# Reordering VectorE's low parts around the gated tiles of a decoder layer's FFN

## The chip, the cores and the metric

The kernel runs on one core of a Trainium2 chip. The metric is the device time of one execution in microseconds (us), given as the median of several runs. PE is TensorE, DVE is VectorE, ACT is ScalarE, POOL is GpSimd, SP is SyncE, whose queue issues nearly all loads. "L176" is line 176 of the kernel.

## The reference

One decoder layer over 256 tokens of width 1024: a mixer (pooling and attention), a cross-attention into 256 memory tokens, and a gated FFN of inner width 2816, each followed by a layer norm of `alpha * h + branch`. The change touches the FFN:

```python
def swiglu(h, w_gate, w_up, w_down):
    return (jax.nn.silu(h @ w_gate) * (h @ w_up)) @ w_down
...
h = layer_norm(DEEPNORM_ALPHA * h + swiglu(h, w_gate[l], w_up[l], w_down[l]), ln3_g[l], ln3_b[l])
```

All data are float32.

## The kernel before

**High and low parts.** TensorE multiplies in a rounded 32-bit type (fp32r). So every operand is cut in two: ACT casts it to fp32r (the high part, `w101h`), DVE subtracts that from the original (the low part, `w101l`), and a product is the sum of three matmuls (L477 high x high, L478 with the low part, L479). A weight tile is 128 x 1024 elements, 512 KB. It goes through a load into one of 7 raw buffers (`w101r`, issued on SP at L108 or L105), ACT's cast (L160) and DVE's subtraction (L176). The raw buffer of tile i is used again by tile i+7, so the load of w108 waits for the low part of w101.

**The stream of weights.** The class `Stream` numbers the tiles in the order of use. `cast()` emits the load, the cast and, unless `apart` is set or the tile is in `lazy`, one low part; what is cast and not yet subtracted waits in `unsplit`. `prepare(upto)` casts up to a tile and subtracts everything below it. `next()` is called after a step of the products and casts one tile more while fewer than `ahead` tiles are in hand (8, then 10 from chunk 3 on) beyond `used`; it does nothing while `held` is set. `get()` asks for the tile that is needed now and looks one tile further. Instructions stand on each engine in the order in which the program emits them: an engine never takes a later one first.

Some tiles are sums of others. A "fourth" tile (w87, w90, w94, w97, w117, ...) is completed by a DVE addition at L165 before it can be cast; sums that are built in DRAM (`sum_z`, `sum_w`, for the down projection) are begun by SP copies (L428, L433) and completed by accumulating DMAs from POOL (`add_first`, `add_second`, L440), in three thirds.

**The FFN's chunks.** The 2816 inner columns are 11 chunks of 256. Chunk c takes four tiles: chunk 1 w69 to w72, chunk 4 w81 to w84, chunk 7 w99 to w102, chunk 8 w103 to w106, chunk 9 w107 to w110, chunk 10 w111 to w114. `proj_both` runs four row blocks of high parts (L492) and then their low parts (L498), twice; 16 steps. Each chunk fills four PSUM banks (`pg`); chunks alternate between two sets of four. After a chunk, `Gated.add` empties them: ACT copies (L1342), DVE adds (L1343, four sums). In the next chunk `multiply` applies silu on ACT and multiplies on DVE (L1348), and `split` makes the gated tile's sum forms on DVE (`add_forms`, L727 to L729), its cast on ACT (L1361) and its low part on DVE (L1366). For the chunks c from 2 to 4 `split` first asks for one more weight tile, whose low part then stands between that cast and L1366.

**The row chunks.** Chunks 5 and 6 (`ROWS`) are computed together from w85 to w98 in 28 products of three matmuls (`Rows.products`) into seven banks. `leave` empties them: an ACT copy (L1445) and then seven DVE operations (L1447 to L1460), all of which follow, directly or not, from L1445. Chunk 7 takes its four banks over from the first four of these. `multiply` (L1464), eight transposes on TensorE (L1473) and `split` (L1479 to L1485) follow inside chunk 7.

**The down projection.** After chunk 10 TensorE multiplies the gated tiles with w115 to w146 (`summed`, two products a tile), and then with w147 to w150 (`pieces`). Its eight banks are those of chunks 9 and 10; the first four products write to banks of chunk 9, the fifth, with w117, to one of chunk 10. At the end DVE combines the sums and does the layer norm (L1001 to L926).

`make_forms` (L1368) prepares sum forms of h2 for the row chunks in seven steps: four DVE operations of 512 columns, two ACT casts (L1382), two DVE subtractions (L1385).

Of the kernel before, what the change touches and what calls it, by code (L numbers as in the profile page):

```python
# [24 lines left out]
NFC = DFF // CW  # L25
# [18 lines left out]
ROWS = (5, 6)  # L44
# [5 lines left out]
def r32(t):  # L50
    return t.bitcast(F32)


class Stream:
# [137 lines left out]
    def next(self):  # L192

        if not self.held:
            self.prepare(min(self.used + self.ahead, len(self.tiles) + 1))

    def get(self, numbers, k):

# [24 lines left out]
def decoder_layer(  # L223
# [26 lines left out]
    ws = Stream(nc, rp, wp)  # L250
# [110 lines left out]
    def split_xt(k, n=2):  # L361
        split(*xT.parts(k, n), xr[:, k:k + n, :])
# [7 lines left out]
    def split_mem(k):  # L370
        split(*mT.parts(k, 4), mr[0][:, k:k + 4, :])
# [70 lines left out]
    def add_first(i):  # L442
        assert i in sums_begun
        js = slice(i * THIRD, (i + 1) * THIRD)
        add_to(sum_z[:, :, js], w_sum[:, 2:4, js])

    def add_second(i):
        assert ~i in sums_begun
        js = slice(i * THIRD, (i + 1) * THIRD)
        add_to(sum_w[:, js], sum_z[:, 1, js])  # L450
# [33 lines left out]
    def proj_both(pss, numbers, yT, group=KD):  # L484

        for k0 in range(0, KD, group):
            for k in range(k0, k0 + group):
                hi, _ = ws.get(numbers, k)  # L490
                for b, ps in enumerate(pss):
                    nc.tensor.matmul(ps, hi[:, b * P:(b + 1) * P], yT.both(k), start=k == 0, stop=False,  # L492
                                     skip_group_check=True)
                yield
            for k in range(k0, k0 + group):
                _, lo = ws.parts_of(numbers, k)
                for b, ps in enumerate(pss):
                    nc.tensor.matmul(ps[:, S:], lo[:, b * P:(b + 1) * P], yT.pair(k)[0], start=False,  # L498
                                     stop=k == KD - 1, skip_group_check=True)
                ws.done(numbers, k)  # L500
                if ws.pace == 1:
                    ws.next()
                yield
# [31 lines left out]
    def run(gen, n=None):  # L535

        while n is None or n > 0:
            if next(gen, gen) is gen:
                return False
            n = None if n is None else n - 1  # L540
        return True

    def split(h, l, ps):
        nc.scalar.copy(h, ps)
        nc.vector.tensor_sub(l, ps, r32(h))
# [5 lines left out]
    def transpose_tok(dst, tok, t, k0, copy=None):  # L551

        ps = bank("tp")
        for k in range(4):
            nc.tensor.transpose(ps[:, k * P:(k + 1) * P], tok[:, (k0 + k) * P:(k0 + k + 1) * P], ident)
        ts = slice(t * P, (t + 1) * P)
        y = ps.rearrange("p (k t) -> p k t", k=4)
        split(*dst.parts(k0, 4, ts), y)
        if copy is not None:
            nc.scalar.copy(copy[:, k0:k0 + 4, ts], y)  # L560
# [164 lines left out]
    def add_forms(q, eng=nc.vector):  # L725

        eng.tensor_sub(q[..., 4:6, :], q[..., 0:2, :], q[..., 1:4:2, :])  # L727
        eng.tensor_sub(q[..., 6, :], q[..., 5, :], q[..., 0, :])
        eng.tensor_add(q[..., 7, :], q[..., 2, :], q[..., 6, :])  # L729
# [508 lines left out]
    products(1, "w", PLAN["w"][1:])  # L1238
    first = shared.parts(0)
    next(first)  # L1240
    xattend(3, homes[1])
    run(first)
# [14 lines left out]
    ws.used += 2  # L1257
    norm.stats()
    next(second)
    norm.unit()  # L1260

# [33 lines left out]
    def gated_parts(c):  # L1295


        if c in SUMMED:
            t = (late if c == ROWS[-1] + 1 else ap).tile([P, 2, 8, P], F32R, tag="a8", name=f"g{c}")
            gT[c] = t[:, 0], t[:, 1]  # L1300
            return
        if not shared:
            shared.append(ap.tile([P, 2, 8, P], F32R, tag="a8", name="go"))
        j = LAST.index(c)
        gT[c] = tuple(shared[0][:, n, 4 * j:4 * j + 4] for n in range(2))
# [14 lines left out]
    def gated_t():  # L1320
        pt = bank("pgt").rearrange("p (f t) -> p f t", f=2)
        for t in range(T):
            for f in range(2):
                nc.tensor.transpose(pt[:, f, t * P:(t + 1) * P], sg0[:, t, f * P:(f + 1) * P], ident)
        gated_parts(0)
        split(gT[0][0], gT[0][1], pt.rearrange("p f (t s) -> p (f t) s", t=T))

    class Gated:
# [18 lines left out]
            nc.scalar.activation(gate, gate, AF.Silu, bias=0.0, scale=1.0)  # L1347
            nc.vector.tensor_mul(gate, gate, up)  # L1348

        def split(self):  # L1350
            gated_parts(self.c)
            hi, lo = gT[self.c]
            q, n = self.forms, 4
            part = ROWS[0] - 3 <= self.c < ROWS[-1]
            if part:
                ws.apart = True
                ws.more()
            if self.c in SUMMED:
                n = 8
                add_forms(q)  # L1360
            nc.scalar.copy(hi[:, :n], q[:, :n])  # L1361
            if part:
                while ws.unsplit:
                    ws.low()
                ws.apart = False
            nc.vector.tensor_sub(lo[:, :n], q[:, :n], r32(hi[:, :n]))  # L1366

    def make_forms():  # L1368

        q = h2f.rearrange("p (j f) (t s) -> p j f t s", f=2, t=2)  # L1370
        at = {(f, t): q[:, :, f, t] for f in range(2) for t in range(2)}
        nc.vector.tensor_sub(at[1, 1], at[0, 1], at[1, 1])
        yield
        nc.vector.tensor_sub(at[0, 1], at[0, 0], at[0, 1])
        yield
        nc.vector.tensor_sub(at[0, 0], at[1, 1], at[0, 0])
        yield
        nc.vector.tensor_add(at[1, 0], at[1, 0], at[0, 0])
        yield
        halves = [[y[:, j:j + 4] for y in (*extra, h2f)] for j in (0, 4)]  # L1380
        for hi, _, y in halves:
            nc.scalar.copy(hi, y)  # L1382
        yield
        for hi, lo, y in halves:
            nc.vector.tensor_sub(lo, y, r32(hi))  # L1385
            yield
# [114 lines left out]
    left, rows, later = None, None, norms[0].vectors()  # L1501
    extra = [pool.tile([P, KD, S], F32R, tag="a8", name=f"extra{i}") for i, pool in enumerate((late, ap))]
    more_forms = make_forms()
    for c in range(1, NFC):
        if c == ROWS[0]:
            run(more_forms)
            rows = Rows()
            ws.lazy = c_gu[ROWS[-1] + 1]
            gu = rows.products()
            run(gu, 3)  # L1510
            left.multiply()
            run(gu, 3)
            left.split()
            run(gu, 10)
            add_first(1)
            add_second(1)
            ws.held = True
            run(gu)
            left = rows
        if c in ROWS:  # L1520
            continue
        pss = [(accbank if c % 2 else bank)("pg") for _ in range(4)]
        if c == 3:
            ws.ahead += 1
            ws.widen("spare", sp)
            add_second(0)
        if c == 7:
            add_first(2)
            add_second(2)
        ws.held = ws.held or c == ROWS[0] - 1  # L1530
        gu = proj_both(pss, c_gu[c], h2T, KD if c == 1 else 4)
        run(gu, 2)
        if left:
            left.multiply()
        run(gu, 2)
        if left and left is rows:
            run(gu, 3)
            left.transposed()
            left.split()
            ws.held = False  # L1540
        elif left:
            left.split()
            run(more_forms, {2: 4, 3: 1}.get(c, 0))
            if c == ROWS[-1] + 2:
                run(later)
        else:
            run(gu, 4)
            gated_t()
        if c >= 2:
            run(gu, 7 if c < ROWS[0] else 4)  # L1550
            if c == 3:
                run(more_forms, 2)
            ws.held = True
        run(gu)
        left = Gated(c, pss)
        left.add()
        ws.held = False
# [174 lines left out]
```

## Time and profile before

| what | value |
|---|---|
| median of 3 runs | 382.34 us (381.67 to 382.8) |
| profiled execution, its own time | 384.75 us |
| its span, first to last instruction | 382.4 us |
| PE / DVE / ACT busy in the span | 367.8 / 342.0 / 230.9 us |
| mean granted TensorE clock | 0.985 |

The profiled execution takes 2.35 us more than its span, and 2.4 us more than the median of the runs. Busy shares are means over the whole kernel; the FFN runs from about 196 us to the end. A row of a timeline gives start, length, engine, line, operation, output<-input, shape and count, and in brackets how long the engine was idle just before and what ended that.

### The profile page before, as it was taken

The numbers are of one execution on the slowest core, as the hardware profiler recorded it, in microseconds if no ns is written. First come the engines' busy times: TensorE is split into PE (matmuls) and PEld (weight loads), VectorE is DVE, ScalarE is ACT, GpSimd is POOL, SyncE is SP. The second block draws the span as 40 slices with busy tenths as digits, with TensorE's granted clock in tenths as the row PEclk, the third lists the DMA queues.
The fourth block names the chain that finished last, engine by engine and source line by source line (L and its number), as shares of the span: only waits on it lengthen the run. The fifth ranks groups of instructions, "written<-read, shape, count | busy, mean of one in ns | idle before, by whom it ended". The sixth has DMA issues, their size and how long they took to land.

```text
span 382.4 us, 5499 instructions
## 1 busy us (share of the span) xinstructions
PE 367.8 (96%) x1941; PEld 311.4 (81%) x1941; DVE 342.0 (89%) x523; ACT 230.9 (60%) x356; POOL 36.5 (10%) x41
## 2 busy tenths in 40 slices
PE   9999999999999999999999999986999995999994
PEld 8888878888888889988888888863888884888882
DVE  6878899998999999999879897989598989899995
ACT  5767768657262965672487446846395467676602
POOL 0000055500130001001100001000100000000013
PEclk9999999999999999999999999999899997999999
DMA  7999997869769999999989489999999757899502
GB/s 273 411 411 362 221 395 237 342 209 300 285 137 258 393 373 317 282 329 366 284 221 366 159 272 316 279 304 316 401 271 333 237 187 220 275 312 295 191 0 110
DMA packets 33754, 107.58 MB, mean 281 GB/s; under 512 B 3264, under 2 KB 4544, under 8 KB 32320
## 3 DMA queue, kind: packets, MB, share of 16 engines
q1 hardware_dynamic: 31056, 93.41, 67.3%
q0 software_dynamic: 2240, 13.37, 17.8%
q10 hardware_dynamic: 432, 0.46, 0.3%
q8 instruction: 15, 0.25, 0.3%
q14 instruction: 11, 0.09, 0.1%
HBM read 106.18 MB, written 27.79 MB: 350 GB/s over the span
## 4 chain that ended last, share of the span: by engine, by line
PE 65%; DVE 20%; issue 5%; DMA 5%; ACT 4%; DVEq 0%; ACTq 0%
PE pg L492 9%; PE m L477 5%; PE m L478 5%; PE m L479 5%; PE pg L498 4%; PE pxk L492 4%; PE pqk L611 4%; DMA w50r<-in_w_xq 3%; PE x L477 2%; PE pxq L492 2%; PE x L478 2%; PE pqk L614 2%; PE x L479 2%; PE pu L492 2%; PE pxk L498 2%
## 5 line engine op out<-in xcount | busy, mean ns | idle before, releaser
L1361 ACT CAST g<-sq 128x1024 fp32r<-128x1024 f32 x7 | 7.4, 1052 | 21.6 <-DVE sq L729 21.6
L916 POOL TENSOR_TENSOR rs<-mv,mhalf 128x1 f32<-128x1 f32 x6 | 4.4, 726 | 125.5 <-DVE mv L914 125.5
L1366 DVE TENSOR_TENSOR g<-sq,g 128x1024 fp32r<-128x1024 f32 x7 | 8.6, 1226 | 6.7 <-ACT g L1361 6.7
L676 ACT ACTIVATE pr<-pr,mx 128x128 f32<-128x128 f32 (+1 forms) x16 | 7.1, 445 | 7.7 <-DVE mx L707 7.7
L440 POOL DMA_DIRECT2D sum_z<-in_w_sum x3 | 3.2, 1056 | 77.1 <-DMA sum_z<-in_w_sum 77.1
L1347 ACT ACTIVATE sq<-sq 128x512 f32<-128x512 f32 x8 | 5.1, 640 | 7.0 <-DVE sq L1343 7.0
L905 DVE BATCH_NORM_STATS2 st<-r 128x6 f32<-128x512 f32 (+1 forms) x12 | 8.1, 672 | 0.4
L570 ACT ACTIVATE h2f<-tp,turned 128x128 f32<-128x128 f32 x8 | 3.0, 456 | 7.0 <-PE tp L567 7.0
L921 DVE SCALAR_TENSOR_TENSOR r<-r,mv,gb 128x512 f32<-128x512 f32 (+2 forms) x10 | 6.9, 724 | 0.1
L727 DVE TENSOR_TENSOR sq<-sq 128x256 f32<-128x256 f32 x9 | 3.8, 423 | 3.3 <-ACT sq L1479 3.2
L1342 ACT COPY sq<-pg 128x256 f32<-128x256 f32 x16 | 5.1, 368 | 2.2 <-PE pg L498 2.2
L1022 DVE TENSOR_TENSOR r<-r,u 128x512 f32<-128x512 f32 x6 | 6.0, 1016 | 0.1
L819 ACT CAST xkTh<-pxk 128x256 fp32r<-128x256 f32 x8 | 2.6, 377 | 5.7 <-PE pxk L498 5.7
L1343 DVE TENSOR_TENSOR sq<-pg,sq 128x256 f32<-128x256 f32 x16 | 6.0, 418 | 0.0
L1343 DVE TENSOR_TENSOR sg<-pg,sg 128x256 f32<-128x256 f32 x16 | 6.0, 418 | 0.0
L932 ACT ACTIVATE h<-r,rs 128x512 f32<-128x512 f32 x2 | 1.3, 718 | 7.3 <-DVE r L921 7.3
L1348 DVE TENSOR_TENSOR sq<-sq,sg 128x512 f32<-128x512 f32 x8 | 5.5, 691 | 0.2
L1027 DVE TENSOR_TENSOR r<-m,r 128x512 f32<-128x512 f32 (+1 forms) x8 | 5.2, 652 | 0.5 <-PE m L479 0.4
L676 ACT ACTIVATE xpr<-xs,mx 128x256 f32<-128x256 f32 x6 | 2.8, 472 | 4.7 <-DVE mx L687 4.7
L776 POOL TENSOR_TENSOR win<-upad 128x542 f32<-128x542 f32 x2 | 4.0, 1992 | 16.9 <-DVE upad L809 16.9
L440 POOL DMA_DIRECT2D sum_w<-sum_z x3 | 2.6, 851 | 29.2 <-DMA sum_z<-in_w_sum 29.2
L1342 ACT COPY sg<-pg 128x256 f32<-128x256 f32 x16 | 5.3, 389 | 0.0
(1373 smaller groups left out, 1398.7 us busy)
## 6 DMA issues: line engine op xcount, KB each, us to landing
sum_z<-in_w_sum SPq DMA_DIRECT2D x3, 1536.0 KB, 9.5
sum_z<-in_w_sum POOLq DMA_DIRECT2D x3, 1536.0 KB, 14.9
sum_w<-in_w_sum SPq DMA_DIRECT2D x3, 768.0 KB, 11.5
sum_w<-sum_z POOLq DMA_DIRECT2D x3, 768.0 KB, 7.9
gs_z<-in_w_gs SPq DMA_DIRECT2D x1, 2048.0 KB, 9.4
gs_z<-in_w_gs POOLq DMA_DIRECT2D x1, 2048.0 KB, 18.1
wr<-in_w_qkv SPq DMA_DIRECT2D x5, 256.0 KB, 4.8
mr<-in_mem_t SPq DMA_DIRECT2D x1, 1024.0 KB, 11.6
```

The costliest lines, as they stand in the source:

```text
L477: nc.tensor.matmul(ps, wa, ya, start=start, stop=False, skip_group_check=part)
L478: nc.tensor.matmul(ps, wa, yb, start=False, stop=False, skip_group_check=part)
L479: nc.tensor.matmul(ps, wb, ya, start=False, stop=stop, skip_group_check=part)
L492: nc.tensor.matmul(ps, hi[:, b * P:(b + 1) * P], yT.both(k), start=k == 0, stop=False, skip_group_check=True)
L498: nc.tensor.matmul(ps[:, S:], lo[:, b * P:(b + 1) * P], yT.pair(k)[0], start=False, stop=k == KD - 1, skip_group_check=True)
L611: nc.tensor.matmul(qk[i], part(i)[0], xT.both(k), start=first, stop=False, skip_group_check=True)
L614: nc.tensor.matmul(qk[i][:, S:], part(i)[1], x_hi, start=False, stop=last, skip_group_check=True)
L676: nc.scalar.activation(dst[:, j, :], src[:, j, :], AF.Exp, bias=mx[:, j:j + 1], scale=sign, accum_out=sm[:, j:j + 1])
L905: nc.vector.bn_stats(self.st[:, self.n, :], self.r[:, c0:c1] if src is None else src)
L1342: nc.scalar.copy(y[:, f, :], ps[:, S:])
L1343: nc.vector.tensor_add(y[:, f, :], ps[:, :S], y[:, f, :])
L1366: nc.vector.tensor_sub(lo[:, :n], q[:, :n], r32(hi[:, :n]))
```

## The change

It has five parts.

- `next()` calls `more()`, which casts a tile without subtracting everything that is left over. So the lazy tiles (chunk 7's w99 to w102) stay `unsplit` until `get` asks for them, which is after the row chunks' sums.
- `split` may be given work to emit between the cast and L1366 (`fill`): steps of `more_forms` in chunks 2 and 3. The seven steps of `more_forms` are spread anew: two in the gap of chunk 1's gated tile and two behind it, the casts late in chunk 2, one subtraction in the gap of chunk 2's gated tile, one late in chunk 3.
- `split` asks for one more tile for c = 2 to 4 and 7 to 9, instead of 2 to 4 alone. In the row chunks `apart` is set one product ahead of the split of chunk 4's gated tile, so that two tiles (w96, w97) can stand there.
- `held` is set through chunk 10 (`NFC - 1`).
- The DMAs that complete the last third of `sum_z` and `sum_w` are emitted at chunk 9 instead of chunk 7.

```diff
     def next(self):
 
         if not self.held:
-            self.prepare(min(self.used + self.ahead, len(self.tiles) + 1))
+            self.more()
...
-        def split(self):
+        def split(self, fill=None):
             gated_parts(self.c)
             hi, lo = gT[self.c]
             q, n = self.forms, 4
-            part = ROWS[0] - 3 <= self.c < ROWS[-1]
+            part = ROWS[0] - 3 <= self.c < NFC - 1
             if part:
                 ws.apart = True
                 ws.more()
...
             nc.scalar.copy(hi[:, :n], q[:, :n])
+            if fill:
+                run(*fill)
             if part:
                 while ws.unsplit:
                     ws.low()
...
             left.multiply()
-            run(gu, 3)
+            run(gu, 5)
+            ws.apart = True
+            run(gu, 1)
             left.split()
-            run(gu, 10)
+            run(gu, 7)
             add_first(1)
             add_second(1)
             ws.held = True
...
-        if c == 7:
+        if c == 9:
             add_first(2)
             add_second(2)
-        ws.held = ws.held or c == ROWS[0] - 1
+        ws.held = ws.held or c in (ROWS[0] - 1, NFC - 1)
...
         elif left:
-            left.split()
-            run(more_forms, {2: 4, 3: 1}.get(c, 0))
+            left.split((more_forms, 4 - c) if c in (2, 3) else None)
+            if c == 2:
+                run(more_forms, 2)
             if c == ROWS[-1] + 2:
                 run(later)
...
             run(gu, 7 if c < ROWS[0] else 4)
-            if c == 3:
-                run(more_forms, 2)
+            if c < ROWS[0] - 1:
+                run(more_forms, 1)
             ws.held = True
```

## Rows read from the trace of the kernel before

**Rows 1.** The page's chain of work that ended last, by engine.
```profile
PE 65%; DVE 20%; issue 5%; DMA 5%; ACT 4%; DVEq 0%; ACTq 0%
```
**Rows 2.** Busy time by stretch: span, each engine, granted clock, DMA share, GB/s.
```profile
236.00:246.00 10.00, 10.00 (x54) 8.59 (x53) 9.83 (x18) 5.78 (x10) 0.09 (x1) 1.00 1.04 271
...
256.00:266.00 10.00, 6.59 (x24) 4.27 (x24) 9.89 (x10) 6.62 (x8) 0.00 (x0) 1.00 0.95 321
266.00:274.00 8.00, 7.35 (x30) 5.71 (x31) 5.36 (x9) 1.23 (x2) 1.04 (x1) 0.79 1.02 411
...
322.00:324.00 2.00, 2.00 (x6) 1.61 (x5) 2.00 (x3) 1.47 (x2) 0.00 (x0) 0.50 1.05 399
```
**Rows 3.** TensorE's timeline, row chunks to the down projection.
```profile
241.58 0.40 PE L477 MATMUL g<-w86h,h2T 128*128 128x512 f32 x1
...
259.98 0.50 PE L478 MATMUL g<-w97l,extra 128*128 128x512 f32 x1 [0.76 <-DVE w97l L176]
...
266.25 0.50 PE L492 MATMUL pg<-h2T,w99h 128*128 128x512 f32 x1 [1.45 <-DVE row L1447]
...
273.77 1.04 PE L1473 MATMUL pgt<-ident,row 128*128 128x128 f32 x8
...
280.69 2.00 PE L492 MATMUL pg<-h2T,w103h 128*128 128x512 f32 x8
...
314.09 0.40 PE L477 MATMUL m<-w115h,g 128*128 128x512 f32 x1
...
320.95 0.80 PE L477 MATMUL m<-w117h,g 128*128 128x512 f32 x1 [3.96 <-DVE sq L1343]
```
**Rows 4.** VectorE's timeline over the same stretch and the end.
```profile
233.41 1.23 DVE L176 TENSOR_TENSOR w87l<-w87r,w87h 128x1024 fp32r<-128x1024 f32 x1 [1.62 <-ACT w87h L160]
...
244.03 0.75 DVE L1343 TENSOR_TENSOR sq<-pg,sq 128x256 f32<-128x256 f32 x2
...
260.97 1.22 DVE L176 TENSOR_TENSOR w99l<-w99r,w99h 128x1024 fp32r<-128x1024 f32 x1
...
265.51 0.69 DVE L1447 TENSOR_TENSOR row<-g,row 128x512 f32<-128x512 f32 x1
...
275.02 0.42 DVE L727 TENSOR_TENSOR sq<-sq 128x256 f32<-128x256 f32 x1 [3.25 <-ACT sq L1479]
...
317.26 0.69 DVE L1366 TENSOR_TENSOR go<-sq,go 128x512 fp32r<-128x512 f32 x1 [0.69 <-ACT go L1361]
...
357.01 1.23 DVE L176 TENSOR_TENSOR w146l<-w146r,w146h 128x1024 fp32r<-128x1024 f32 x1
...
369.52 0.69 DVE L1027 TENSOR_TENSOR r<-m,r 128x512 f32<-128x512 f32 x1 [0.43 <-PE m L479]
...
375.33 0.43 DVE L905 BATCH_NORM_STATS2 st<-acc 128x6 f32<-128x256 f32 x1 [0.18 <-PE acc L479]
```
**Rows 5.** Groups by line: VectorE's L1366, with the idle time ahead of it.
```profile
L1366 DVE TENSOR_TENSOR g<-sq,g 128x1024 fp32r<-128x1024 f32 x7 | 8.6, 1226 | 6.7 <-ACT g L1361 6.7
```
**Rows 6.** Busy time of all engines between two VectorE instructions of group 4.
```profile
244.03:375.33 131.30, 123.15 (x591) 102.16 (x590) 119.71 (x158) 77.85 (x98) 5.69 (x6) 0.96 0.78 255
```
**Rows 7.** SyncE's queue: the load of w102.
```profile
256.88 0.33 SPq L108 DMA_DIRECT2D w102r<-in_w_gu  x1
```
**Rows 8.** Tile w102r, from issue to landing.
```profile
DMA to landing us min/median/max: 4.2/4.2/4.2
```
**Rows 9.** ScalarE's timeline: the cast that L1445 stands behind.
```profile
262.36 1.04 ACT L160 CAST w102h<-w102r 128x1024 fp32r<-128x1024 f32 x1
```
**Rows 10.** Tile w146l: TensorE's matmuls, the two numbers are first and last start.
```profile
L478 PE MATMUL m<-w146l,g x2: 389/389/389, 361.4 to 362.1; 128*128 128x512 f32 x2
```
**Rows 11.** Tensor sum_w, 280 to 300 us: starts and time to landing.
```profile
L440 POOL DMA_DIRECT2D sum_w<-sum_z x1: 852/852/852, 286.1 to 286.1; - x1
L105 SPq DMA_DIRECT2D w117r<-sum_w x1: 326/326/326, 290.7 to 290.7; - x1
...
DMA to landing us min/median/max: 8.0/8.7/9.3
```

## The prediction

> **What bounds the kernel now.** I began with the chain of waits: TensorE holds 65% of it, VectorE 20% [rows 1]. That mean mixes two states, so I cut the FFN into stretches [rows 2]. Up to 256 us TensorE is never idle, while VectorE is busy 9.83 of 10 us and the DMA engines 1.04 of their time. From 256 to 274 TensorE is busy only 13.9 of 18 us; VectorE runs 9.89 of 10 us in the first part of that and then, from 266, has little to do. So the bound passes to VectorE and back. TensorE's own timeline names the waits [rows 3]: low parts in the row chunks (one of four stands, 0.76 us; all four 2.26), then chunk 7's second bank, 1.45 us, for L1447, and at 317 the largest, 3.96 us, where the fifth product of the down projection waits for chunk 10's sums. After each group the granted clock falls to 1.2 GHz: 0.79 on the mean of 266 to 274 is 3.4 us at half rate (8 x 0.21 / 0.5), and 0.50 at 322 to 324 [rows 2].
>
> The important reading is behind that. In the down projection TensorE does not wait at all, but VectorE is only just ahead: w146's low part ends at 358.2 and TensorE reads it at 361.4, 3.2 us later [rows 4, 10]. At the end VectorE waits for TensorE 0.43 and 0.18 us [rows 4]. So TensorE can come forward by some 3 us on its own; everything beyond that must come from VectorE. **I therefore make the sum on VectorE**, from chunk 4's sums (244.03) to the last L905 (375.33): 131.3 us, of which 119.7 busy [rows 4, 6]. The other 11.6 us are waits. The instructions between are the same before and after; only their order changes, so the busy part stays.
>
> **The change part by part.**
>
> *The start of the sum.* Ahead of 244.03 two of L1366's waits (1.1 each: 6.7 us in six of seven, [rows 5]) are filled with L1372/L1374 and with one L1385, and w87h no longer stands behind two casts (L1382), which cost VectorE 1.62 us [rows 4]. That is 3.8 us, but chunk 4's sums cannot begin before TensorE ends chunk 4, 241.58 [rows 3]. Between 241.6 and 242.0 (one ACT copy later) I take 241.7. Gain 2.33, with 1.5 us of slack behind it, so this term is firm.
>
> *The gaps of L1366 after it.* Four of the six remain before: chunks 4, 7, 8 and 10, 4.5 us. By the counters, chunk 4's gap gets w96l and w97l (95 tiles of the limit 99 are cast, two fit), and chunk 7's w111l (111 of 113). Chunk 8's gets nothing: 117 tiles are cast, the limit is 117. Chunk 10's is outside the new range. So 2.2 us go and 2.2 stay. Chunk 9's smaller tile waits 0.69 [rows 4], and with w119l in the gap this goes too.
>
> *Chunk 7's low parts behind the row sums.* Before, w99l to w102l take 260.97 to 265.51 and L1447 comes right after [rows 4]. Now L1447 needs only L1445, but ACT has the casts w99h to w102h ahead of it in its order. VectorE will be through with w98l at about 257.7 (the start 2.3 earlier, chunk 4's gap filled, w99l to w102l gone). When can w102h end? ACT's four casts, 0.95 each, cannot start before 255.6, which gives 259.4 and L1447 at 260.0. The load bounds it from above: w102 lands at 261.1 before (256.88 + 4.2, [rows 7, 8]) and is cast at 262.36 [rows 9]; its raw buffer now comes free at 251.4, but the DMA engines are full from 236 on (1.04, 0.95 [rows 2]), so the bytes ahead of it move forward only as far as the loads began earlier, about 1.2 us. An unmoved landing gives L1447 at 262.7. I take 260.7, hence **3.0 us of new wait** (2.4 to 5.1), a part of it already at L165 of w97. TensorE then ends the row products near 262.6 instead of 264.4 and finds its banks free.
>
> *What is late next.* w99l, w100l now stand behind the seven sums, w101l and w102l behind the row chunks' own split (L1485). TensorE waits for each: about 0.7, 1.4, 1.8 and 0.2 us. VectorE in turn waits once, between w100l and L727: TensorE's block of w100l (0.5), four transposes and ACT's copy (273.77 to 275.02, 1.25 [rows 3, 4]), 1.8 us with 0.2 inside, instead of 3.25 and 0.19. Chunk 7 ends near 278.5 (before 280.69). If the clock falls here as it did before, the 0.9 us of matmuls on this path take 1.8; I put half of that in the sum, 0.4.
>
> *Loads.* The load of w108 needs w101l, now at 276.6; it and five more are issued within 8 us beside the accumulation. The similar burst before landed in about 6 us a tile. I allow 0.6 us of VectorE waiting in chunk 8 (0 to 1.5). One wait of 0.35 for w90h, behind four copies on ACT.
>
> *No casts in chunk 10.* Its sums follow chunk 9's go tile directly. TensorE runs 33.4 us from 280.69 to 314.09 for three chunks [rows 3], so it starts the down projection near 311.9; VectorE reaches the sums at 313.4 and ends them by 314.7, just when the fifth product needs them (311.9 + 4 x 0.68). The 3.96 us and the half rate behind it (13 matmuls at 0.43 instead of 0.23, 2.6 us) go for TensorE. But w120l to w122l, which stood ahead, now come after. TensorE would be 2.2 + 4.0 + 2.6 = 8.8 us ahead of before, and VectorE less.
>
> *The late DMAs.* On POOL nothing stands between them and the second third, so being emitted two chunks later does not delay them; their source copies come about 4 us later, and the sums of that third are needed only in the second half of the down projection, which hides it. Nothing.
>
> **The sum.** Old waits that I can name: 4.5 (L1366) + 3.25 + 0.19 + 0.69 + 0.43 + 0.18 and three small ones, 0.76, = 10.0 of the 11.6; the remaining 1.6 are gaps of a tenth, which stay. New waits: 3.0 + 1.8 + 0.4 + 0.6 + 0.35 + 2.2 = 8.35. Gain 2.33 + 10.0 - 8.35 = **4.0 us**: last L905 at 371.4, span 378.4, and the profiled execution 380.8 instead of 384.75. The median lies 2.4 under the profiled execution: 382.34 - 4.0 = **378.4 us**. With all bounds at their bad end new waits are 11.8 and the gain 0.5; at the good end 6.8 and 5.6. TensorE's 8.8 less VectorE's 4.0 exceeds the lead of 3.2, so it will wait some 1.6 us for low parts in the down projection, and VectorE will end the kernel.
>
> **The rivals.**
>
> *Late loads.* w102 lands no earlier than before, and the clock falls: L1447 at 262.7, the transposes at half rate, chunk 8's loads 1.5 late. Gain 0.5 to 1.2: 381.4. For it: the full DMA engines. Against: the loads ahead of it start 1.1 us earlier, by the first filled gap.
>
> *TensorE falls back in the down projection.* It now waits for low parts there in short pieces. Each fall like the one at 321 loses 2.6 us; VectorE's end leaves it some 3 us, so two falls cost 2: 380.4. Against: waits of 2.3 us in four pieces between 255 and 261 left the clock at full rate until 266; only with 1.45 more did it fall. The Trainium skill (TensorE: Matmul & The Clock Gate, "HAM oscillation — how this bites in real kernels") describes a loop that falls back to half rate at every wait between its bursts; by that rule this rival would be the outcome, and the two falls in this trace agree in kind, the four short waits do not.
>
> *VectorE is not the bound.* If the waits before L1447 and before L727 vanish (3.0 + 1.8), VectorE gains 8.8 as TensorE does: 373.7. It needs the loads 3 us earlier than the full DMA engines seem to allow.
>
> *Slower: the accumulations wait for reads.* The reads of `sum_z` for w118 and w121 are now emitted ahead of the last third's accumulation. If the two are ordered by the whole tensor and not by its parts, POOL waits for w121r (near 302), then the two DMAs follow (9.3 us for the second [rows 11]; the first has twice its bytes, so between 9.3 and 18.6, I take 14) and end at 325, and w124r, read after that, reaches L165 8 us late: 382.3 - 4 + 8 = 386.5. Against: w117r was issued at 290.7 while an accumulation into another third, issued at 286.1 and 9.3 long, was under way [rows 11].
>
> *The gaps are not filled.* If no tile is free when `split` asks, 2.2 us return: 380.6. The counters say otherwise.
>
> **How the numbers follow.** My forecast, a gain of 1.2 to 6, 0.66; late loads 0.13; TensorE falling back 0.08; VectorE not the bound 0.07; slower by the accumulations 0.04; gaps unfilled 0.02. About 0.3% (1.15 us) is what a measurement of this kernel tells from no change. Faster: 0.66 + 0.07 + 0.07 + 0.02, and a little of the late loads, 0.83. The same: the rest of them, 0.11. Slower 0.06. The range must take in the falls, the unfilled gaps and half of the late loads: 375.9 to 381.2.
>
> **What would show it.** Right: w96l and w97l between L1361 and L1366 of chunk 4; L1447 before w99l, at 260 to 262, after an idle VectorE; no wait at the fifth product of the down projection; TensorE waiting there later for low parts; the last L905 without a wait for TensorE. Wrong: VectorE idle behind L165 of w97 or L1447 for more than 5 us, w109 to w111 cast late, or a second stretch of 0.50 after 312.

## The result and the profile after

| | before | after |
|---|---|---|
| median | 382.57 us (381.67 to 383.93, 4 runs) | 387.64 us (386.26 to 387.91, 4 runs) |
| profiled execution, its span | 384.75, 382.4 | 386.26, 384.0 |
| mean granted clock | 0.985 | 0.992 |

The ratio is 1.0122, 95% interval 1.0083 to 1.0161: the changed kernel is slower by 1.2%, where 378.4 and "faster" were forecast. The two profiled spans differ by 1.6 us only, the medians by 5.1. The profiled execution of before is above its median, that of after below its own. This matters further down.

In the code after the change, lines behind the cast L1361 are two higher: L1366 is L1368, the row chunks' L1445 and L1447 are L1447 and L1449, L1479 is L1481.

VectorE's timeline after, over the stretch of [rows 4]:

```profile
241.60 0.75 DVE L1343 TENSOR_TENSOR sq<-pg,sq 128x256 f32<-128x256 f32 x2 [1.31 <-ACT sq L1342]
...
252.23 0.69 DVE L165 TENSOR_TENSOR w97r<-w96r,w97r 128x512 f32<-128x512 f32 x1 [0.68 <-DMA w97r<-gs_w]
...
260.25 0.69 DVE L1449 TENSOR_TENSOR row<-g,row 128x512 f32<-128x512 f32 x1 [1.81 <-ACT row L1447]
...
270.48 0.42 DVE L727 TENSOR_TENSOR sq<-sq 128x256 f32<-128x256 f32 x1 [1.89 <-ACT sq L1481]
...
287.59 1.22 DVE L176 TENSOR_TENSOR w108l<-w108r,w108h 128x1024 fp32r<-128x1024 f32 x1 [3.23 <-ACT w108h L160]
...
292.57 1.22 DVE L176 TENSOR_TENSOR w109l<-w109r,w109h 128x1024 fp32r<-128x1024 f32 x1 [3.15 <-ACT w109h L160]
...
303.57 1.23 DVE L176 TENSOR_TENSOR w114l<-w114r,w114h 128x1024 fp32r<-128x1024 f32 x1 [0.24 <-ACT w114h L160]
...
311.82 1.23 DVE L1368 TENSOR_TENSOR g<-sq,g 128x1024 fp32r<-128x1024 f32 x1 [1.12 <-ACT g L1361]
...
330.16 1.22 DVE L1368 TENSOR_TENSOR g<-sq,g 128x1024 fp32r<-128x1024 f32 x1 [1.12 <-ACT g L1361]
...
376.95 0.41 DVE L905 BATCH_NORM_STATS2 st<-acc 128x6 f32<-128x256 f32 x1
```

Up to 287 nearly everything is as forecast: the sums of chunk 4 at 241.60, the row sums at 260.25, the wait of 1.9 us before L727. The gaps of chunks 4 and 7 are filled as counted (w96l and w97l, w111l). Then two low parts, w108l and w109l, wait 3.23 and 3.15 us for casts. Before, neither waited at all:

```profile
286.55 1.23 DVE L176 TENSOR_TENSOR w108l<-w108r,w108h 128x1024 fp32r<-128x1024 f32 x1
...
288.29 1.23 DVE L176 TENSOR_TENSOR w109l<-w109r,w109h 128x1024 fp32r<-128x1024 f32 x1
```

The last L905 has no wait in brackets: VectorE, not TensorE, brings up the end, as forecast, but at 376.95 and not 371.4.

TensorE's timeline after, the places of [rows 3]:

```profile
258.50 0.50 PE L478 MATMUL g<-w98l,extra 128*128 128x512 f32 x1 [1.09 <-DVE w98l L176]
...
268.65 0.74 PE L498 MATMUL pg<-h2T,w100l 128*128 128x256 f32 x4 [1.13 <-DVE w100l L176]
...
276.28 1.21 PE L498 MATMUL pg<-h2T,w101l 128*128 128x256 f32 x8 [1.87 <-DVE w101l L176]
...
278.46 2.00 PE L492 MATMUL pg<-h2T,w103h 128*128 128x512 f32 x8
...
305.18 3.59 PE L492 MATMUL pg<-h2T,w111h 128*128 128x512 f32 x8 [4.29 <-DVE sq L1343]
...
318.20 0.40 PE L477 MATMUL m<-w115h,g 128*128 128x512 f32 x1
...
320.95 0.39 PE L477 MATMUL m<-w117h,g 128*128 128x512 f32 x1
```

Chunk 7 ends at 278.46 (278.5 forecast), 2.2 us earlier than before. The fifth product of the down projection (w117) waits for nothing any more, so this part of the change did what it says. But chunk 10 now stops for 4.29 us at its first matmul, whose bank waits for chunk 8's sums, and the down projection starts at 318.20, against 314.09 in [rows 3].

Busy time by stretch, after (columns as in [rows 2]: span, PE, PEld, DVE, ACT, POOL, granted clock, DMA share, GB/s):

```profile
260.00:268.00 8.00, 6.83 (x33) 5.23 (x31) 7.44 (x11) 1.45 (x3) 0.00 (x0) 1.00 0.28 93
...
275.00:281.00 6.00, 4.72 (x28) 4.14 (x29) 6.00 (x7) 4.62 (x8) 1.04 (x1) 1.00 0.69 128
281.00:290.00 9.00, 9.00 (x56) 8.12 (x55) 5.19 (x8) 1.58 (x2) 0.00 (x0) 1.00 1.02 304
...
305.00:311.00 6.00, 5.82 (x19) 4.62 (x20) 5.60 (x11) 2.32 (x4) 0.00 (x0) 0.72 0.87 267
```

The same view of the kernel before, its first stretch:

```profile
260.00:268.00 8.00, 5.98 (x22) 3.88 (x23) 7.89 (x9) 4.26 (x6) 0.00 (x0) 1.00 0.95 319
```

Here is the place. From 260 to 268 the DMA engines are busy 0.28 of their time, where before it was 0.95. The transfers that are not made there, loads and source copies together, come to (319 - 93) GB/s x 8 us = 1.8 MB, as much as 3.4 weight tiles of 512 KB. They are owed, and from 281 on the engines are full again while VectorE is busy only 5.19 of 9 us.

Tile w109r, on SP's queue and from issue to landing, after:

```profile
L108 SPq DMA_DIRECT2D w109r<-in_w_gu x1: 433/433/433, 277.4 to 277.4; - x1
...
DMA to landing us min/median/max: 14.0/14.0/14.0
```

The chain of waits after, one piece of it (start, length):

```profile
284.39 18.00 DMA w114r<-in_w_gu
```

w109 is issued at 277.4 and lands 14.0 us later, at 291.4; its cast follows at once and VectorE's low part at 292.57. One load, w114's, is 18 us of the chain: 5% of the span. In the time in question POOL's two accumulating DMAs of the last third run too: the one into `sum_z` is issued at 275.28, the one into `sum_w` at 290.79.

### The profile page after: what moved, and what is told of

Same layout as the page of the kernel before. It is cut to its first block, busy times and chain, and to the rows that moved or that the text cites. A ratio compares the mean times of both kernels' runs of the same rounds, so it can differ in the third digit from the quotient of the medians.

```text
span 384.0 us, 5494 instructions
## 1 busy us (share of the span) xinstructions
PE 365.3 (95%) x1941; PEld 309.1 (80%) x1941; DVE 341.9 (89%) x523; ACT 230.9 (60%) x356; POOL 36.4 (9%) x41
## 4 chain that ended last, share of the span: by engine, by line
PE 70%; DVE 14%; DMA 8%; ACT 3%; issue 3%; DVEq 0%; ACTq 0%
PE pg L492 9%; DMA w114r<-in_w_gu 5%; PE pg L498 5%; PE m L478 4%; PE m L479 4%; PE pxq L492 4%; PE pxk L492 4%; PE m L477 4%; PE pqk L611 4%; PE x L477 2%; PE x L478 2%; PE x L479 2%; PE pxk L498 2%; PE pxq L498 2%; PE pu L492 2%
## 5 line engine op out<-in xcount | busy, mean ns | idle before, releaser
L1361 ACT CAST g<-sq 128x1024 fp32r<-128x1024 f32 x7 | 7.4, 1052 | 13.9 <-DVE sq L729 13.9
L1368 DVE TENSOR_TENSOR g<-sq,g 128x1024 fp32r<-128x1024 f32 x7 | 8.6, 1223 | 2.2 <-ACT g L1361 2.2
L905 DVE BATCH_NORM_STATS2 st<-r 128x6 f32<-128x512 f32 (+1 forms) x12 | 8.1, 672 | 0.4
L492 PE MATMUL pg<-h2T,w111h 128*128 128x512 f32 x8 | 3.6, 623 | 4.3 <-DVE sq L1343 4.3
L1343 DVE TENSOR_TENSOR sq<-pg,sq 128x256 f32<-128x256 f32 x16 | 6.0, 416 | 1.4 <-ACT sq L1342 1.3
L492 PEld LDWEIGHTS pg<-h2T,w111h 128*128 128x128 f32 x8 | 2.3, 285 | 5.1 <-DVE sq L1343 4.5
L1343 DVE TENSOR_TENSOR sg<-pg,sg 128x256 f32<-128x256 f32 x16 | 5.9, 412 | 0.0
L727 DVE TENSOR_TENSOR sq<-sq 128x256 f32<-128x256 f32 x9 | 3.8, 420 | 2.0 <-ACT sq L1481 1.9
```

What stands on the lines that cost most here:

```text
L905: nc.vector.bn_stats(self.st[:, self.n, :], self.r[:, c0:c1] if src is None else src)
L1343: nc.vector.tensor_add(y[:, f, :], ps[:, :S], y[:, f, :])
```

## The experiments

Two theories stood at the start. **Contention:** the loads of w108 to w114 are slow because they fall together with the accumulations and their source copy. **Lateness:** they are issued late, because w99 to w102 hold four of the seven raw buffers until their low parts are done. A third reading was that VectorE isn't the bound at all, so that TensorE's 4.29 us set the time.

### e1: after, without the accumulations of the last third

```diff
-        if c == 9:
-            add_first(2)
-            add_second(2)
```

> The changed kernel without the two POOL accumulations into the last third of sum_z and sum_w; that third then lacks these operands. Theory (the delayed loads of w108 to w114 share the DMA engines with these accumulations): the loads land in 4 to 7 us instead of 10 to 18, VectorE's waits for w108h and w109h (3.2 and 3.2 us) shrink below 1 us in sum, TensorE's 4.3 us at chunk 10's first bank go, and the time is 380 to 382. Rival (seven loads issued in 8 us are too many by themselves): landings stay over 10 us and the time at 386 or more.

Measured: 381.22 us (379.88 to 381.99), ratio to before 0.9952 (0.9934 to 0.9970), inside the expected 380 to 382. Tile w109r in e1, on SP's queue and to landing:

```profile
L108 SPq DMA_DIRECT2D w109r<-in_w_gu x1: 431/431/431, 277.8 to 277.8; - x1
...
DMA to landing us min/median/max: 8.0/8.0/8.0
```

Two rows of VectorE's timeline in e1:

```profile
286.86 1.23 DVE L176 TENSOR_TENSOR w109l<-w109r,w109h 128x1024 fp32r<-128x1024 f32 x1 [0.43 <-ACT w109h L160]
...
371.27 0.41 DVE L905 BATCH_NORM_STATS2 st<-acc 128x6 f32<-128x256 f32 x1
```

The load is issued at the same time as in after and lands in 8.0 us instead of 14.0 (w110 to w113 in 8.2 to 8.6; 4 to 7 had been expected). The two waits of 3.2 us become one of 0.43, TensorE's wait in chunk 10 is gone, and the last L905 comes at 371.27. The forecast, whose sum had no such waits, said 371.4. The source copies still run in e1. So the accumulations are what made these loads slow.

### e2: after, with the last third's source copies begun a chunk earlier

```diff
-    for i, (at, then) in enumerate((..., (c_gu[9][0], c_gu[9][2]))):
+    for i, (at, then) in enumerate((..., (c_gu[8][0], c_gu[8][2]))):
```

> The changed kernel with the copies that begin the last third of sum_z and sum_w emitted ahead of w103 and w105 instead of w107 and w109, so that copies and accumulations fall where the DMA engines are idle (260 to 278 us). Theory (contention): w108 to w113 land in 5 to 8 us, VectorE waits under 1 us for them, time 377.5 to 380.5, faster than both kernels. Rival (the traffic only moves the delay to w101 to w106 and to the row sums): the first row sum starts after 262 us, and the time is 383 or more.

Measured: 382.47 us (381.04 to 384.14), ratio 0.9991 (0.9972 to 1.0010). That is 5 us better than after, but the expectation is missed. The rival's sign did not come either: the first row sum starts at 260.93. The accumulations start at 263.50 and 278.09. The second of them still lies beside the same loads: w109 to w113 land in 9.6 to 10.3 us, and w109's low part waits 2.03 us (3.15 after, 0.43 in e1). The last L905 comes at 372.99, 1.7 later than in e1. Moving the accumulations takes away most of the collision, not all.

### e3: after, with the low parts of chunk 7 ahead of the row sums again

```diff
-            ws.lazy = c_gu[ROWS[-1] + 1]
```

> The changed kernel without the lazy tiles: the low parts of w99 to w102 stand ahead of the row sums again, all else as changed. Theory (VectorE sets the end, and putting these four behind the sums only moved its wait and held back the raw buffers): loads of w106 to w109 are issued by 264 us, no wait for w108h or w109h, TensorE waits again for the row sums' banks, and the time is 376 to 379. Rival (TensorE's wait for the banks and the half rate behind it set the time): 380.5 to 383.

Measured: 379.01 us (378.13 to 380.03), ratio 0.9905 (0.9886 to 0.9923), at the upper edge of what was expected. TensorE waits again for the row sums' banks, 1.44 us. Tile w109r in e3:

```profile
L108 SPq DMA_DIRECT2D w109r<-in_w_gu x1: 1126/1126/1126, 263.0 to 263.0; - x1
...
DMA to landing us min/median/max: 15.1/15.1/15.1
```

Two rows of VectorE's timeline in e3:

```profile
285.76 1.23 DVE L176 TENSOR_TENSOR w110l<-w110r,w110h 128x1024 fp32r<-128x1024 f32 x1 [0.43 <-ACT w110h L160]
...
368.88 0.41 DVE L905 BATCH_NORM_STATS2 st<-acc 128x6 f32<-128x256 f32 x1
```

The load of w109 is no faster here (15.1 us), but it is issued at 263.0 instead of 277.4, and so lands at 278.1. No low part waits for it. All accumulations run. So neither theory holds alone: a slow landing that is begun 14 us earlier costs nothing (e3), and a late issue without the accumulations costs 0.43 us (e1); the change made both meet. e3 is also 2.4 us ahead of e1 on VectorE: the wait of 1.80 before the row sums is not there, L727 waits 1.68 instead of 1.89, and the stretch starts 0.38 earlier. The lazy part costs these 2 us even without any collision.

### e4: before, with no casts in chunk 10

```diff
-        ws.held = ws.held or c == ROWS[0] - 1
+        ws.held = ws.held or c in (ROWS[0] - 1, NFC - 1)
```

> The kernel before with one part of the change alone: no casts in chunk 10. Theory (VectorE sets the end): TensorE's 4.0 us wait at the fifth product of the down projection and the half rate after it go, but VectorE's work is only reordered, so no more than 0.3 to 1.5 us come of it: 381 to 382. Rival (TensorE sets the end): 376 to 379.

Measured: 382.50 us (381.30 to 383.47), ratio 0.9992 (0.9977 to 1.0006): no gain is shown, where 381 to 382 was expected. Two waits of TensorE's timeline in e4:

```profile
326.14 0.50 PE L477 MATMUL m<-w124h,g 128*128 128x512 f32 x1 [1.20 <-ACT w124h L160]
327.59 0.67 PE L478 MATMUL m<-w124l,g 128*128 128x512 f32 x1 [0.95 <-DVE w124l L176]
```

A row of VectorE's timeline in e4:

```profile
273.45 0.43 DVE L727 TENSOR_TENSOR sq<-sq 128x256 f32<-128x256 f32 x1 [1.68 <-ACT sq L1479]
```

The wait of 3.96 us at the fifth product, the largest that TensorE has in [rows 3], is gone, 2.15 us of it come back at w124, and the time is the same. The last L905 of e4 waits for nothing. So VectorE is the bound there, as the sum assumed. The row of L727 tells something else: its 1.68 us stand against 3.25 in [rows 4], though up to there the two programs are the same.

### e5: e3, with all gaps of L1368 filled

```diff
-            part = ROWS[0] - 3 <= self.c < NFC - 1
+            part = ROWS[0] - 3 <= self.c < NFC
...
-            left.split((more_forms, 4 - c) if c in (2, 3) else None)
+            left.split((more_forms, 4 - c) if c in (2, 3) else (later, 2) if c == 9 else None)
...
-            if c == ROWS[-1] + 2:
+            if c == ROWS[-1] + 3:
                 run(later)
```

Chunk 8's gap gets two operations of a layer norm that stand elsewhere otherwise, chunk 10's the low part of w125.

> As e3_no_lazy (low parts of chunk 7 ahead of the row sums), and the last two gaps between a gated tile's cast and its low part filled as well: two of the four norm operations L949/L951 in chunk 8's, one weight tile (w125) in chunk 10's. Theory (VectorE sets the end, so each idle microsecond taken from it shows): two waits of 1.1 us go, 376.5 to 378, that is 1 to 2.5 us under e3_no_lazy. Rival (TensorE or the loads set the end by now): no change against e3_no_lazy, 378.5 to 379.5.

Measured: 381.43 us (380.20 to 383.12), ratio 0.9970 (0.9951 to 0.9989): missed. ScalarE's timeline in e5:

```profile
304.82 1.05 ACT L1361 CAST g<-sq 128x1024 fp32r<-128x1024 f32 x1 [7.26 <-PE pg L498]
```

VectorE's row behind it in e5:

```profile
305.90 1.23 DVE L1368 TENSOR_TENSOR g<-sq,g 128x1024 fp32r<-128x1024 f32 x1 [4.15 <-ACT g L1361]
```

The cast of gated tile 8 waits 7.26 us for TensorE's chunk 10, and L1368 behind it 4.15 instead of 1.11. A norm operation that is put off holds its gain-and-bias tile longer, and then gated tile 8 would get another buffer, one that TensorE still reads; this reading of the 7.26 us was not tested. What is shown is that filling this gap with these operations makes a larger wait than the one it fills.

### e6: e3, with casts in chunk 10 as before

```diff
-        ws.held = ws.held or c in (ROWS[0] - 1, NFC - 1)
+        ws.held = ws.held or c == ROWS[0] - 1
```

> As e3_no_lazy, but with casts in chunk 10 as before. Theory (with VectorE some 5 us ahead, TensorE's 4 us wait for chunk 10's sums and the half rate after it would now come to be the later of the two): 380 to 382. Rival (holding chunk 10 is worth nothing, as in e4_hold10 alone): 378.5 to 379.5.

Measured: 380.30 us (378.40 to 381.50), ratio 0.9937 (0.9916 to 0.9958), as expected. TensorE's wait at the fifth product is back (2.88 us), and so is VectorE's of 0.69 before the small gated tile. The same line that is worth nothing in e4 is worth 1.3 us here. That is little more than the noise, as the two intervals (e3: 0.9886 to 0.9923) just overlap, but the last L905 agrees: 370.39 in e6, 368.88 in e3.

### e7: before, with the lazy low parts and the late accumulations alone

```diff
         if not self.held:
-            self.prepare(min(self.used + self.ahead, len(self.tiles) + 1))
+            self.more()
...
-        if c == 7:
+        if c == 9:
             add_first(2)
             add_second(2)
```

> The kernel before with one part of the change alone: chunk 7's low parts behind the row sums (and with it the two late DMAs emitted at chunk 9); no gap filled, chunk 10 not held. Theory (it holds the raw buffers back, so that the loads of w108 to w114 fall on the accumulations): these loads take 10 us or more, VectorE waits 5 us or more for them, and the time is 386 to 390. Rival (the slow loads come of the parts together, not of this one): 381 to 384.

Measured: 393.70 us (392.20 to 393.76), ratio 1.0273 (1.0246 to 1.0300): the direction is right, the loss larger than expected. The largest wait of VectorE's timeline in e7:

```profile
297.24 1.22 DVE L176 TENSOR_TENSOR w109l<-w109r,w109h 128x1024 fp32r<-128x1024 f32 x1 [8.20 <-ACT w109h L160]
```

And the largest of TensorE's in e7:

```profile
310.52 3.78 PE L492 MATMUL pg<-h2T,w111h 128*128 128x512 f32 x8 [6.68 <-DVE sq L1343]
```

One wait of 8.20 us for w109, whose load took 15.8 us, and 6.68 us of TensorE behind it. These two parts of the change together make the whole loss and more, and the other parts bring time. The late accumulations without the lazy part are in e3, which loses nothing; the lazy part with the accumulations emitted at chunk 7, as before, was not run.

### e8 and e9: e3, with chunk 10's gap filled, and with chunk 8's too

```diff
-            part = ROWS[0] - 3 <= self.c < NFC - 1
+            part = ROWS[0] - 3 <= self.c < NFC
```

That is e8. For e9 the casts of chunk 9 are also held until the split, so that w115's low part is free to stand in chunk 8's gap:

```diff
-        ws.held = ws.held or c in (ROWS[0] - 1, NFC - 1)
+        ws.held = ws.held or c in (ROWS[0] - 1, NFC - 2, NFC - 1)
...
+            if c == NFC - 2:
+                ws.held = False
```

> The kernel e3_no_lazy, with the gap of chunk 10 filled too: the low part of w125 stands between that chunk's gated cast and its low part. Theory (VectorE sets the end, and each wait taken off it shortens the program by its own length): the 1.1 us wait behind the cast of gated tile 10 goes and no other takes its place; 377.5 to 378.5 against the 379.0 of e3_no_lazy. Rival (TensorE or a load is the bound by then, or another wait takes its place): 378.7 to 379.5, with the last of VectorE's sums no earlier than the 368.9 of e3_no_lazy.

> The kernel e8_fill_10, with the gap of chunk 8 filled as well, by the low part of w115: the casts of chunk 9 are held until the split of gated tile 8 is emitted, so a low part of a weight tile and no norm operation stands in the gap, unlike in e5_fill_all. Theory: both 1.1 us waits go; 376.5 to 378. Rival: as in e5_fill_all another wait takes their place (TensorE waits for a weight tile of chunk 9, or ScalarE's cast of gated tile 8 is late); 378.5 or more.

Measured: e8 377.10 us (376.22 to 379.10), ratio 0.9865 (0.9839 to 0.9890), a little better than expected; e9 378.05 us (376.67 to 378.85), ratio 0.9882 (0.9861 to 0.9903), just above what was expected. e8 is the fastest kernel of this study. Its last L905 is at 366.99, 1.89 earlier than in e3: besides the gap's 1.1 us, the 0.43 of w110's low part is not there. In e9 all seven waits of L1368 are gone, but the time is not better than e8's. The page's chain by engine for e9:

```profile
PE 86%; DVE 5%; DMA 4%; ACT 1%; POOL 1%; issue 1%; POOLq 0%; DVEq 0%; ACTq 0%
```

In [rows 1] TensorE had 65% of the chain. In e9 it waits for nothing from 265 us to the end of its work for the down projection. That alone does not make it the bound, because VectorE does not wait for it either. Two rows of VectorE's timeline in e9:

```profile
271.75 0.42 DVE L727 TENSOR_TENSOR sq<-sq 128x256 f32<-128x256 f32 x1 [3.03 <-ACT sq L1481]
...
312.83 1.23 DVE L176 TENSOR_TENSOR w120l<-w120r,w120h 128x1024 fp32r<-128x1024 f32 x1 [0.35 <-ACT w120h L160]
```

The first of these waits is 1.64 us in e8, the second is not there. So e9 gains 1.12 us in chunk 8's gap and loses 1.39 + 0.35 = 1.74 at these two places: 0.6 us behind, and its last L905 is at 367.64, 0.65 later than in e8. VectorE's own waits account for the difference, and the two engines are about level here. The larger loss, at L727, stands behind transposes of TensorE that fell into a time at half rate. Busy time in the stretch 264 to 274, in e8:

```profile
264.00:274.00 10.00, 9.61 (x53) 7.97 (x53) 7.72 (x15) 4.23 (x6) 1.04 (x1) 1.00 1.01 376
```

The same stretch in e9:

```profile
264.00:274.00 10.00, 10.00 (x48) 8.35 (x49) 6.33 (x14) 3.40 (x6) 1.04 (x1) 0.83 1.03 388
```

The profiled execution of e9 also lost some 1.7 us here to half rate (10 x 0.17 / 0.5 = 3.4 us at 1.2 GHz instead of 2.4), that of e8 did not. Whether e9 would be ahead with equal clocks is open; the two intervals overlap.

## Why the prediction was wrong

**The step that failed** is "Loads": "The similar burst before landed in about 6 us a tile. I allow 0.6 us of VectorE waiting in chunk 8 (0 to 1.5)". It cost 3.23 + 3.15 + 0.24 = 6.6 us. The burst that it was compared with (w110 to w113 of before, issued 280.8 to 284.2) falls on the end of one accumulation, issued at 272.51 and landed 13.2 us later, and the start of the next, issued at 286.1. The right one stood in the same trace. Tiles w109r and w112r of the kernel before:

```profile
L108 SPq DMA_DIRECT2D w109r<-in_w_gu x1: 573/573/573, 265.6 to 265.6; - x1
...
DMA to landing us min/median/max: 13.8/13.8/13.8
...
L108 SPq DMA_DIRECT2D w112r<-in_w_gu x1: 328/328/328, 283.1 to 283.1; - x1
...
DMA to landing us min/median/max: 6.2/6.2/6.2
```

w109 was under way from 265.6 to 279.4, beside the accumulation issued at 272.51, and took 13.8 us; before, nobody waited for it. It was issued behind both source copies too (262.60 and 264.93), so not all of its time is the accumulation's; the comparison of after and e1 is the cleaner one. With 14 us instead of 6 the forecast's own time for these loads, from 276.6 on, puts w109 some 8 us later, and no cover of that length was there. The same mistake stands in "The late DMAs": only their own results' due time was looked at ("hides it. Nothing"), not what they do to the loads beside them. The Trainium skill (DMA: Bandwidth & Descriptors, "Issuing engines are not separate DMA queues") says that transfers issued by different engines run on the same 16 DMA engines and interleave. The trace agrees: SP's load of w109 took 14.0 us beside POOL's accumulation and 8.0 without it (e1).

**The other terms on VectorE** came out, each from the rows above. Start of the sums: 241.60 for 241.7. Waits before the row sums: 0.68 + 1.81 = 2.5 for 3.0. Before L727: 1.89 + 0.18 for 1.8. w90: 0.36 for 0.35. Gaps of chunks 8 and 10: 2.24 for 2.2. Half rate in chunk 7: nothing for 0.4. Loads: 6.6 for 0.6. Together the named waits are 13.8 for 8.35, and the excess of 5.4 us is nearly all of the 5.55 by which the last L905 missed 371.4. With the collision taken away it comes to 371.27 (e1). That it lies so close to 371.4 is in part luck: in e1 the sums start 0.45 us earlier than forecast, and smaller errors the other way cancel it.

**The second error, from the profile to the median.** On the profiled executions the miss is 386.26 - 380.8 = 5.5 us, on the medians 387.64 - 378.4 = 9.2. The other 3.8 us come from "The median lies 2.4 under the profiled execution", which was carried over to the new kernel: its median lies 1.4 above. The profiled execution of before, 384.75, is slower than all four of its runs in the table. In e1 the collision is gone and the same error is left: its span is 378.1 (378.4 forecast) and its profiled execution 380.17 (380.8), but its median is 381.22 (378.4). A part of it can be named. L727's wait of 3.25 us [rows 4] holds 1.6 us of a clock fall that e4, with the same program up to there, did not have. The sum counted this as time to be won, though the median of before may not contain it. The rest stays open.

**VectorE as the bound: right** for before and after (e4, and the end without a wait for TensorE). It stays right as VectorE's waits are taken out; in e9 the two engines are about level.

**No casts in chunk 10: right**: no wait at the fifth product, low parts waited for later (w125l 0.35 us and w146l 0.77, 1.1 for the 1.6 forecast). What the prediction did not see is that chunk 10's first matmul would take over the wait, 4.29 us. VectorE's lateness is its cause: the wait is for L1343, it is gone in e1, and the last L905 does not wait for TensorE.

**The rivals.** None of the slower ones was what happened. "Late loads" had the right place with 1.5 us in chunk 8, and L1447 late and the clock down besides, which were not so. "TensorE falling back" in the down projection: no; the granted clock from 312 to 377 was 1.00. The waits of 0.69 to 1.87 us between 258 and 277 left the clock at 1.00; behind the 4.29 us at 305 it fell (0.72 from 305 to 311). The loop that the prediction named (the Trainium skill, TensorE: Matmul & The Clock Gate, "HAM oscillation — how this bites in real kernels") falls back behind each wait of some 3 to 5 us for a load. The 4.29 us agree with that; for the shorter waits of this rival that loop decides nothing, and the prediction took it too far. "Accumulations ordered by the whole tensor": POOL's second one waited 14.47 us, but for its source copy, not for a read. The accumulations did decide the sign, through the DMA engines. (This rival's sum, 382.3 - 4 + 8, gives 386.3 and not 386.5.)

One of the signs set down as "wrong" came, "w109 to w111 cast late".

## What to carry to other kernels

When low parts or other last readers of a load buffer are put off, count the loads that their buffers hold back, and look where those loads will fall. Take their landing time from a row with the same neighbours, not from a burst that looks alike. Make the sum against a profiled execution, but check with a second one which of its waits every execution has.

## What the runs showed of the hardware

**Beside an accumulating DMA the engines moved less without looking idle.** From 275 to 281 the engines moved 274 GB/s in before, at a share of 1.06, and 223 GB/s in e3, at 1.04, both while the accumulation into `sum_z` was under way (issued at 272.51 and 269.8, landed 13.2 and 14.5 us later); from 281 to 290 in e1, without one, 384 GB/s at a share of 1.00. The rate is not low for the whole of an accumulation: in e3 the stretch from 281 to 290, with the end of this one and the start of the next, has 370 GB/s at 1.04. Why the rate falls is not shown, and for a part of the time from 275 to 281 a source copy into `sum_w` was under way as well. The share alone does not tell how fast a load will be.

**The same waits do not always bring the clock down.** In before and e4 the programs and TensorE's waits up to 267 are the same (0.76 at w97, 1.45 or 1.46 at w99). From 266 to 274 the granted clock was 0.79 [rows 2] in the one and 1.00 in the other. e8 and e9 differ in the same way, with waits of 1.31, 1.45 and 0.29 us against 1.27, 1.45 and 0.29. In e7 the clock fell earlier, to 0.79 on the mean of 260 to 268, behind four waits (0.94, 0.39, 0.76, 0.17) that stand in before too, within 0.01 us, and left its clock at 1.00 up to 266 [rows 2]. So a sum should carry such a fall as a chance, here of some 1.6 us, and not as a fixed cost or gain.
